# Inverse roots of GroupNorm (all groups) and of the last block's LayerNorm (in a column) with variance and running product in PSUM

## The chip, the cores and the metric

The kernel runs on one core of a Trainium2 chip. The metric is the device time of one execution in microseconds (us). Below, PE is TensorE, DVE is VectorE, ACT is ScalarE, POOL is GpSimd, and SP is SyncE, which issues the DMAs. Each engine works through its own list of instructions in order; an instruction waits until the semaphores that it needs are set, and everything behind it on that engine waits with it.

## What is computed

One block of a sequence model (2048 tokens, 1024 channels) with two token mixers, of which three things matter here:

```
h = rmsnorm(x) * (1 + scale) + shift
p = h @ w_in                                   # all inputs of both mixers
# mixer A: u = causal conv(val * sigmoid(gate)), then LayerNorm over the 1024 channels of a token
u = (u - mean(u)) * rsqrt(var(u) + LN_EPS) * ln_g + ln_b
y_conv = (silu(u) * silu(og)) @ w_conv_out
# mixer B: RWKV-7 scan per head of 64 channels, then GroupNorm over the 64 channels of a head and token
o = (o - mean(o)) * rsqrt(var(o) + GN_EPS) * gn_g + gn_b
y_rwkv = ((o + bonus) * silu(r_og)) @ w_rwkv_out
m = sigmoid(g_conv) * y_conv + sigmoid(g_rwkv) * y_rwkv
out = rmsnorm(x + gate * (m @ w_out))
```

The change concerns the two `rsqrt` of LayerNorm and GroupNorm.

## The kernel before

**Tiling and stages.** The 2048 tokens are worked in NB = 4 blocks of TB = 512, and the heads of mixer B in 4 groups of four heads, so that there are 16 groups of tokens and heads. A big fp32 product is three passes of 128x128x512 matmuls: each operand is split into a high and a low part (`h_hi`, `h_lo`, `w_hi`, `w_lo`, `w_c`; all write the tile `ps_main`), and hi x hi, lo x hi and hi x lo are summed. The `w_in` product of all blocks comes first and lasts until about 2150 us. Beside it run, block by block, the conv and its LayerNorm, and for each group a scan chain on PE, ACT and DVE (`group`, L1160: tiles `As`, `Tn`, `uv`, `xo`, `S`), then that group's GroupNorm. The three output products (`ro` for mixer B, `co` for mixer A, `o` for `w_out`) come last and are done by a fast matrix scheme (`wino`, L1910): seven products of half-size operands, in the order 0, 1, 6, 4, 2, 3, 5, whose operands are sums of tiles (`cells<-cells`, then `h_lo<-cells,h_hi`; for weights `w_c<-w_raw,w_c`) and whose results are added into `mr`, `mrh` and `cells` (`mr<-ps_main,mr`, `mr<-fc,mr`). While the last groups are still in their chains, PE is filled with the `ro` product of the first two blocks.

**What sets the order.** A planner in the same file runs while the kernel is built. Tasks are generators that `yield` conditions; `note` (L118 to L185) keeps a model of when each engine, tile and DMA will be free, and the next instruction of every engine is chosen from that. So the order of each engine is fixed before the kernel runs, and a change of one step moves others far from it. In the model, DVE and POOL exclude each other when the DVE instruction has more than one input in SBUF, or is a fast copy or `tensor_scalar` from SBUF to SBUF (`both_`).

**The steps that the change touches.** `rsteps` (L380) is the inverse root: a first guess by integer arithmetic on the bits, then three rounds of Newton's method with three DVE instructions each (y*y, times -x/2, plus 1.5 times y). `rsqrt` (L392) runs it at once with a temporary `rs_t`. In GroupNorm (end of `group`, from L1348) the four tokens-by-heads columns give a 128x16 tile of variances `gst`; L1370 calls `rsqrt(rs, st, lt, nc.vector)` with `rs` = `grs`, and POOL then multiplies `uv` by `grs`; PE transposes the result (`late<-ident,uv`), and after the gates it goes to DRAM. In the LayerNorm of the last block (`lnorm_first`, L1468), `ones @ qs` (`late<-lnq,ones`) puts the sum over channels into all 128 rows, so that the root works on a 128x512 tile in which all rows are the same (`lnr`, `lnt`, `lnq`); it is stored to `rl_d` and loaded again later by `last_u` (L2126), which normalizes the last block with it. All recorded instructions carry the line of one helper, L196, so one goes by the names of tiles. `aux` and `late` are PSUM tiles: `late` has one bank (L671), `aux` rotates over two.

Of the kernel before, what the change touches and what calls it, by code (L numbers as in the profile page):

```python
# [9 lines left out]
F32 = mybir.dt.float32  # L10
F32R = mybir.dt.float32r
I32 = mybir.dt.int32
AF = mybir.ActivationFunctionType
ALU = mybir.AluOpType
# [4 lines left out]
P = 128  # L19
D = 1024  # L20
KT = D // P
TB = 512
NTT = TB // P
# [5 lines left out]
RMS_EPS, LN_EPS, GN_EPS, L2_EPS = 1e-6, 1e-5, 64e-5, 1e-12  # L29
# [30 lines left out]
AHEAD = 0.7  # L60
# [24 lines left out]
def hybrid_block(ctx: ExitStack, tc: tile.TileContext, x, x_t, vecs, convk, w2a2, final_g, ada, w_in, w_co, w_ro, w_o, crow, out,  # L85
                 seq=2048, groups=(0, 1, 2, 3), phase2=True, dbg=None):
    NB = seq // TB
# [167 lines left out]
    def ok(*aps):  # L255
        ks = [key(a) for a in aps]
        return lambda: max(ready[q] for q in ks)
# [5 lines left out]
    def idle(name, us):  # L263
        return lambda: vt[name] - us
# [4 lines left out]
    def bank(tag, n=1):  # L269

        def f():
            for t_, past in tags.items():
                if t_.startswith(tag + "_"):
                    free_ = sorted((max(ready.get(q, 0.0), used.get(q, 0.0)) for q in past), reverse=True)
                    m = BANKS[tag] - n
                    return free_[m] if len(free_) > m else 0.0
            return 0.0

        return f

    def both(*ws):

        def f():
            r = [w() for w in ws]
            return None if None in r else max(r)

        return f

    def burst(*ws):
        w = both(*ws)  # L290

        def f():
            r = w()
            if r is None:
                return r
            return r + lag[0]

        return f
# [59 lines left out]
    u_dram = scratch("u_d")  # L358
    xT_dram = scratch("xT")
    xrow_d = [dp.tile([TB], F32, name=f"xrow{b}", tag=f"xrow{b}") for b in range(NB)]  # L360
    rl_d = dp.tile([P, TB], F32, name="rl_d", tag="rl_d")

    grow_d = dp.tile([D], F32, name="grow_d", tag="grow_d")

# [15 lines left out]
    def rsteps(y, x_, t, eng=None):  # L380
        eng = eng or nc.vector
        eng.tensor_scalar(out=y.bitcast(I32), in0=x_.bitcast(I32), scalar1=-0.5, scalar2=float(0x5F3759DF),
                          op0=ALU.mult, op1=ALU.add)
        for _ in range(3):
            yield
            eng.tensor_tensor(out=t, in0=y, in1=y, op=ALU.mult)
            yield
            eng.scalar_tensor_tensor(out=t, in0=t, scalar=-0.5, in1=x_, op0=ALU.mult, op1=ALU.mult)
            yield
            eng.scalar_tensor_tensor(out=y, in0=t, scalar=1.5, in1=y, op0=ALU.add, op1=ALU.mult)  # L390

    def rsqrt(y, x_, pool, eng, t=None):  # L392
        if t is None:
            t = pool.tile(list(x_.shape), F32, name="rs_t", tag="rs_t")
        for _ in rsteps(y, x_, t, eng):
            pass
# [763 lines left out]
    def group(G, before):  # L1160
# [201 lines left out]
        for half in range(2):  # L1362
# [2 lines left out]
            nc.scalar.activation(Dm.rearrange("p (a b) n -> p a b n", a=2), O16[:, half * 2:half * 2 + 2], AF.Square)  # L1365
            yield ok(Dm)
            nc.vector.tensor_reduce(out=st[:, half * 8:half * 8 + 8], in_=Dm, axis=AX.X, op=ALU.add)
        nc.vector.tensor_scalar(out=st, in0=st, scalar1=1.0 / 64, scalar2=GN_EPS, op0=ALU.mult, op1=ALU.add)
        yield idle("DVE", AHEAD + 0.1)
        rsqrt(rs, st, lt, nc.vector)  # L1370
        yield ok(rs)
        nc.gpsimd.tensor_tensor(out=O16, in0=O16, in1=bc(rs), op=ALU.mult)
        yield ok(uv)
# [94 lines left out]
    def lnorm_first(b, hx, ys=None):  # L1468

        def yload(j):  # L1470
            yj = hx.take("lny")
            nc.sync.dma_start(yj, y_dram[b][j])
            if b + 1 == NB:
                ready[key(yj)] += SLACK
            return yj

        eng = nc.vector if b + 1 == NB else nc.gpsimd
        if ys is None:
            yield hx.room(3, 1)
            ys, nxt = yload(0), yload(1)  # L1480
            for j in range(1, KT):
                yj = nxt
                if j + 1 < KT:
                    yield hx.room(1, 1)
                    nxt = yload(j + 1)
                yield ok(ys, yj)
                eng.tensor_tensor(out=ys, in0=ys, in1=yj, op=ALU.add)
                hx.give(yj)
        yield burst(ok(ys), free, bank("late"))
        ps = pl.tile([P, TB], F32, name="late", tag="late")  # L1490
        nc.tensor.matmul(ps, ones, ys, start=True, stop=True)
        mean = ys
        nc.scalar.copy(mean, ps)
        yield hx.room(2, 1)
        nxt, qs = yload(0), None
        for j in range(KT):
            yj = nxt
            if j + 1 < KT:
                yield hx.room(1, 1)
                nxt = yload(j + 1)  # L1500
            yield ok(yj, mean)
            eng.tensor_tensor(out=yj, in0=yj, in1=mean, op=ALU.subtract)
            yield both(ok(yj), hx.room(1))
            yq = hx.take("lnq")
            nc.scalar.activation(yq, yj, AF.Square)
            nc.sync.dma_start(y_dram[b][j], yj)
            hx.give(yj)
            if j == 0:
                qs = yq
            else:  # L1510
                yield ok(yq)
                eng.tensor_tensor(out=qs, in0=qs, in1=yq, op=ALU.add)
                hx.give(yq)
        yield burst(ok(qs), free, bank("late"))
        ps = pl.tile([P, TB], F32, name="late", tag="late")
        nc.tensor.matmul(ps, ones, qs, start=True, stop=True)
        nc.vector.tensor_scalar(out=qs, in0=ps, scalar1=LN_EPS, scalar2=None, op0=ALU.add)
        yield hx.room(2, 1)
        rl, rt = hx.take("lnr"), hx.take("lnt")
        for n, _ in enumerate(rsteps(rl, qs, rt)):  # L1520
            if n % 3 == 0:
                yield idle("DVE", AHEAD + 0.1)
        hx.give(qs, rt)
        hx1.give(mean)
        if b + 1 == NB:
            yield ok(rl)
            nc.sync.dma_start(rl_d, rl)
            hx.give(rl)
            return

        for j in range(KT):
            yield hx.room(3, 1)
            yj, ct, th = yload(j), hx.take("lnc"), hx.take("lnth")
            nc.sync.dma_start(ct, co_dram[b][j])
            yield ok(yj, rl)
            eng.tensor_tensor(out=yj, in0=yj, in1=rl, op=ALU.mult)
            yield ok(yj)
            nc.scalar.activation(th, yj, AF.Tanh, scale=hlg[:, j:j + 1], bias=hlb[:, j:j + 1])
            nc.scalar.activation(yj, yj, AF.Identity, scale=vc("conv_ln_g", j), bias=vc("conv_ln_b", j))
            yield ok(yj)  # L1540
            nc.vector.scalar_tensor_tensor(out=yj, in0=th, scalar=1.0, in1=yj, op0=ALU.add, op1=ALU.mult)
            hx.give(th)
            yield ok(yj, ct)
            eng.tensor_tensor(out=yj, in0=yj, in1=ct, op=ALU.mult)
            hx.give(ct)
            yield ok(yj)
            nc.sync.dma_start(u_dram[b][j], yj)
            hx.give(yj)
        hx.give(rl)
# [192 lines left out]
    with tc.manual_schedule():  # L1742
# [383 lines left out]
        def last_u():  # L2126
            yield when(lambda: side[1].done and turn[0] >= 2)
            yield uc.room(4)
            rl = uc.take()
            nc.sync.dma_start(rl, rl_d)  # L2130
            for j in range(KT):
                yield uc.room(3)
                yt, ct, th = [uc.take() for _ in range(3)]
# [174 lines left out]
```

## Time and profile before

| | us |
|---|---|
| three runs | 2682.25, 2669.76, 2681.33; median 2681.33 |
| the profiled execution | 2679.79 |
| its span in the trace | 2677.9 |
| PE busy in the span | 2591.1 (97%) |
| DVE busy | 2177.5 (81%) |
| POOL busy | 1330.8 (50%), with nothing after about 2250 |
| ACT busy | 1191.8 (45%) |

The share of the span is an average over stages. PE is what bounds most of the run, and what a change can win is in the places where PE stands idle. PE's granted clock is shown as a share of full speed: 1.00 is full, and it falls after a pause.

### The profile page before, as it was taken

The numbers are of one execution on the slowest core, as the hardware profiler recorded it, in microseconds if no ns is written. First come the engines' busy times: TensorE is split into PE (matmuls) and PEld (weight loads), VectorE is DVE, ScalarE is ACT, GpSimd is POOL, SyncE is SP. The second block draws the span as 40 slices with busy tenths as digits, with TensorE's granted clock in tenths as the row PEclk, the third lists the DMA queues.
The fourth block names the chain that finished last, engine by engine and source line by source line (L and its number), as shares of the span: only waits on it lengthen the run. The fifth ranks groups of instructions, "written<-read, shape, count | busy, mean of one in ns | idle before, by whom it ended". The sixth has DMA issues, their size and how long they took to land. (4 is left out here: it accounts for less than half of the span.)

```text
span 2677.9 us, 50719 instructions
## 1 busy us (share of the span) xinstructions
PE 2591.1 (97%) x18328; PEld 2082.4 (78%) x18328; DVE 2177.5 (81%) x3645; ACT 1191.8 (45%) x2315; POOL 1330.8 (50%) x1828
## 2 busy tenths in 40 slices
PE   8999999999999999999999999999999998999997
PEld 6777887777877888788888877878887776778786
DVE  6796889788879887878698878888888698898687
ACT  6444454543434434434444433434444454456443
POOL 3585848462658383827573756493727484000000
PEclk9999999999999999999999999999999998999999
DMA  9888778786787688967877878786766778798974
GB/s 365 293 311 303 252 260 300 246 282 229 245 278 243 223 287 262 323 204 267 281 251 233 283 258 262 224 316 207 266 197 213 241 261 299 248 328 309 349 270 159
DMA packets 390693, 711.59 MB, mean 266 GB/s; under 512 B 137493, under 2 KB 141929, under 8 KB 390442
## 3 DMA queue, kind: packets, MB, share of 16 engines
q1 hardware_dynamic: 390442, 708.35, 78.0%
q8 instruction: 144, 2.36, 0.3%
q14 instruction: 107, 0.88, 0.1%
HBM read 493.82 MB, written 213.26 MB: 264 GB/s over the span
## 5 line engine op out<-in xcount | busy, mean ns | idle before, releaser
L196 PE MATMUL ps_main<-h_hi,w_lo 128*128 128x512 f32 x2304 | 924.6, 401 | 5.2 <-POOL w_lo L196 3.8
L196 PE MATMUL ps_main<-h_hi,w_hi 128*128 128x512 f32 x2304 | 923.3, 401 | 4.9 <-DMA w_hi<-kh_in 4.2
L196 PE MATMUL ps_main<-h_lo,w_hi 128*128 128x512 f32 x2304 | 923.1, 401 | 0.0
L196 DVE SCALAR_TENSOR_TENSOR acc<-u,ck,acc 128x512 f32<-128x512 f32 x928 | 698.9, 753 | 26.8
L196 PEld LDWEIGHTS ps_main<-h_hi,w_hi 128*128 128x128 f32 x2304 | 434.7, 189 | 103.4 <-issue 10.7
L196 PEld LDWEIGHTS ps_main<-h_hi,w_lo 128*128 128x128 f32 x2304 | 434.9, 189 | 103.0 <-issue 5.7
L196 PEld LDWEIGHTS ps_main<-h_lo,w_hi 128*128 128x128 f32 x2304 | 434.8, 189 | 92.8 <-issue 5.3
L196 PE MATMUL ps_main<-h_hi,w_c 128*128 128x512 f32 x896 | 290.2, 402 | 7.9 <-DVE mr L196 4.7
L196 POOL TENSOR_TENSOR itmp<-La,TT 128x126 f32<-128x126 f32 (+22 forms) x496 | 205.3, 414 | 46.3 <-issue 13.2
L196 POOL TENSOR_TENSOR TT<-TT,itmp 128x126 f32<-128x126 f32 (+22 forms) x496 | 204.8, 413 | 38.8
L196 ACT ACTIVATE th<-ps_main 128x512 f32<-128x512 f32 x160 | 95.5, 597 | 281.0 <-PE ps_main L196 255.4
L196 PEld LDWEIGHTS ps_main<-h_hi,w_c 128*128 128x128 f32 x896 | 171.0, 191 | 51.1 <-issue 4.3
L196 PE MATMUL ps_main<-h_lo,w_c 128*128 128x512 f32 x448 | 180.5, 403 | 13.8 <-DVE h_lo L196 13.7
L196 POOL TENSOR_TENSOR w_lo<-w_st,w_hi 128x1024 fp32r<-128x1024 f32 x57 | 137.9, 2419 | 102.0 <-ACT w_hi L196 86.4
L196 ACT COPY uv<-xo 64x256 f32<-64x256 f32 (+1 forms) x192 | 80.9, 438 | 208.4 <-PE xo L196 153.6
L196 DVE SCALAR_TENSOR_TENSOR S<-xo,pe,Se 64x64 f32<-64x64 f32 x512 | 123.1, 280 | 49.0 <-PE xo L196 38.1
L196 PE MATMUL ps_main<-w_c,h_hi 128*128 128x512 f32 x448 | 140.0, 393 | 0.0
L196 ACT CAST w_c<-w_raw 128x512 fp32r<-128x512 f32 x168 | 102.3, 619 | 73.5 <-DMA w_raw<-wk_o 28.9
L196 DVE TENSOR_TENSOR As<-aux,maskA 128x512 f32<-128x512 f32 x128 | 82.4, 686 | 49.4 <-PE aux L196 48.8
L196 PEld LDWEIGHTS ps_main<-h_lo,w_c 128*128 128x128 f32 x448 | 85.8, 192 | 35.3 <-DVE h_lo L196 16.1
L196 ACT ACTIVATE Se<-S,pe 128x128 f32<-128x128 f32 x256 | 88.7, 395 | 40.1 <-DVE S L196 38.8
L196 ACT ACTIVATE t<-ps_main,mu 128x512 f32<-128x512 f32 x96 | 65.8, 686 | 80.3 <-PE ps_main L196 80.0
(301 smaller groups left out, 4525.4 us busy)
## 6 DMA issues: line engine op xcount, KB each, us to landing
w_hi<-kh_in SPq DMA_DIRECT2D x219, 512.0 KB
w_lo<-kl_in SPq DMA_DIRECT2D x219, 512.0 KB
w_st<-w_in_t SPq DMA_DIRECT2D x73, 512.0 KB
kh_in<-w_hi SPq DMA_DIRECT2D x70, 512.0 KB
kl_in<-w_lo SPq DMA_DIRECT2D x70, 512.0 KB
lny<-y_d SPq DMA_DIRECT2D x80, 256.0 KB
w_raw<-wk_o SPq DMA_DIRECT2D x56, 256.0 KB
ada_st<-ada_t SPq DMA_DIRECT2D x16, 512.0 KB
```

What stands on the lines that cost most here:

```text
L196: r = f(*a, **k)
```

## The change

A new `proot` does the same three rounds with ten DVE instructions, all in a row, with x and the temporary t in PSUM and only y in SBUF: each of the three-operand steps then has at most one input in SBUF. In all 16 GroupNorms the variance is written into a bank of `aux`, and the step waits for that bank. In the last block's LayerNorm the sum over channels is taken the other way round: four matmuls with the squares as weights and two columns of ones give [128 tokens, 2] each, so the variance is a 128x4 column and the root works on 4 elements a row where it had 512. A transpose, an ACT copy and a DMA put it into `rl_d` as 512 numbers, and the later load spreads them to all rows.

```diff
--- before.py
+++ after.py
@@ -358,7 +358,7 @@
     u_dram = scratch("u_d")
     xT_dram = scratch("xT")
     xrow_d = [dp.tile([TB], F32, name=f"xrow{b}", tag=f"xrow{b}") for b in range(NB)]
-    rl_d = dp.tile([P, TB], F32, name="rl_d", tag="rl_d")
+    rl_d = dp.tile([TB], F32, name="rl_d", tag="rl_d")
 
     grow_d = dp.tile([D], F32, name="grow_d", tag="grow_d")
 
@@ -388,6 +388,14 @@
             eng.scalar_tensor_tensor(out=t, in0=t, scalar=-0.5, in1=x_, op0=ALU.mult, op1=ALU.mult)
             yield
             eng.scalar_tensor_tensor(out=y, in0=t, scalar=1.5, in1=y, op0=ALU.add, op1=ALU.mult)
+
+    def proot(y, x_, t):
+        nc.vector.tensor_scalar(out=y.bitcast(I32), in0=x_.bitcast(I32), scalar1=-0.5, scalar2=float(0x5F3759DF),
+                                op0=ALU.mult, op1=ALU.add)
+        for _ in range(3):
+            nc.vector.scalar_tensor_tensor(out=t, in0=y, scalar=-0.5, in1=x_, op0=ALU.mult, op1=ALU.mult)
+            nc.vector.tensor_tensor(out=t, in0=t, in1=y, op=ALU.mult)
+            nc.vector.scalar_tensor_tensor(out=y, in0=t, scalar=1.5, in1=y, op0=ALU.add, op1=ALU.mult)
 
     def rsqrt(y, x_, pool, eng, t=None):
         if t is None:
@@ -1365,9 +1373,11 @@
             nc.scalar.activation(Dm.rearrange("p (a b) n -> p a b n", a=2), O16[:, half * 2:half * 2 + 2], AF.Square)
             yield ok(Dm)
             nc.vector.tensor_reduce(out=st[:, half * 8:half * 8 + 8], in_=Dm, axis=AX.X, op=ALU.add)
-        nc.vector.tensor_scalar(out=st, in0=st, scalar1=1.0 / 64, scalar2=GN_EPS, op0=ALU.mult, op1=ALU.add)
-        yield idle("DVE", AHEAD + 0.1)
-        rsqrt(rs, st, lt, nc.vector)
+        yield both(idle("DVE", AHEAD + 0.1), bank("aux"))
+        pg = pa.tile([P, 2, TB // 2], F32, name="aux", tag="aux")
+        gx = pg[:, 0, 0:16]
+        nc.vector.tensor_scalar(out=gx, in0=st, scalar1=1.0 / 64, scalar2=GN_EPS, op0=ALU.mult, op1=ALU.add)
+        proot(rs, gx, pg[:, 1, 0:16])
         yield ok(rs)
         nc.gpsimd.tensor_tensor(out=O16, in0=O16, in1=bc(rs), op=ALU.mult)
         yield ok(uv)
@@ -1511,6 +1521,28 @@
                 yield ok(yq)
                 eng.tensor_tensor(out=qs, in0=qs, in1=yq, op=ALU.add)
                 hx.give(yq)
+        if b + 1 == NB:
+            yield burst(ok(qs), free, bank("late"))
+            ps = pl.tile([P, TB], F32, name="late", tag="late")
+            for tt in range(NTT):
+                nc.tensor.matmul(ps[:, 2 * tt:2 * tt + 2], qs[:, tt * P:tt * P + P], ones[:, 0:2], start=(tt == 0),
+                                 stop=(tt == NTT - 1), skip_group_check=True)
+            st = e2.tile([P, 5, NTT], F32, name="ss0", tag="ss0", bufs=1)
+            vs, rs, t_ = ps[:, 128:128 + NTT], st[:, 3, :], ps[:, 256:256 + NTT]
+            nc.vector.tensor_scalar(out=vs, in0=ps[:, 0:2 * NTT:2], scalar1=LN_EPS, scalar2=None, op0=ALU.add)
+            hx.give(qs)
+            hx1.give(mean)
+            proot(rs, vs, t_)
+            yield burst(ok(st), free, bank("late"), hx.room(1, 1))
+            pt = pl.tile([P, TB], F32, name="late", tag="late")
+            nc.tensor.transpose(pt[0:NTT, 0:P], rs, ident)
+            gt = hx.take("gt")
+            nc.scalar.copy(gt[0:NTT, 0:P], pt[0:NTT, 0:P])
+            yield ok(gt)
+            nc.sync.dma_start(rl_d.rearrange("(n p) -> n p", p=P), gt[0:NTT, 0:P])
+            hx.give(gt)
+            return
+
         yield burst(ok(qs), free, bank("late"))
         ps = pl.tile([P, TB], F32, name="late", tag="late")
         nc.tensor.matmul(ps, ones, qs, start=True, stop=True)
@@ -1522,12 +1554,6 @@
                 yield idle("DVE", AHEAD + 0.1)
         hx.give(qs, rt)
         hx1.give(mean)
-        if b + 1 == NB:
-            yield ok(rl)
-            nc.sync.dma_start(rl_d, rl)
-            hx.give(rl)
-            return
-
         for j in range(KT):
             yield hx.room(3, 1)
             yj, ct, th = yload(j), hx.take("lnc"), hx.take("lnth")
@@ -2127,7 +2153,7 @@
             yield when(lambda: side[1].done and turn[0] >= 2)
             yield uc.room(4)
             rl = uc.take()
-            nc.sync.dma_start(rl, rl_d)
+            nc.sync.dma_start(rl, rl_d.unsqueeze(0).broadcast_to([P, TB]))
             for j in range(KT):
                 yield uc.room(3)
                 yt, ct, th = [uc.take() for _ in range(3)]
```

The planner puts many instructions in other places. First, DVE at the root of the last block's LayerNorm. Before, it lies among the adds of the `ro` product (`mr<-ps_main,mr`) and the steps of the last group's chain (`uv<-xo,uv`, `S<-xo,pe,Se`):

```order
L196 TENSOR_SCALAR lnq<-late 128x512
L196 TENSOR_SCALAR lnr<-lnq 128x512
L196 TENSOR_TENSOR mr_5_24020<-ps_main,mr_9_24024 128x512
L196 SCALAR_TENSOR_TENSOR S_438<-xo,pe,Se 64x64 x4
L196 TENSOR_TENSOR lnt<-lnr 128x512
L196 SCALAR_TENSOR_TENSOR lnt<-lnt,lnq 128x512
L196 SCALAR_TENSOR_TENSOR lnr<-lnt,lnr 128x512
L196 TENSOR_TENSOR mr_6_24021<-ps_main,mr_10_24025 128x512
```

and after, in the chain of the group ahead of it, eleven instructions of 128x4 in a row (the next rows go on in the same way; `ss` is the column y):

```order
L196 TENSOR_TENSOR lnq<-lnq 128x512
L196 TENSOR_TENSOR uv<-xo,uv 64x256
L196 TENSOR_SCALAR late<-late 128x4
L196 TENSOR_SCALAR ss_24058<-late 128x4
L196 SCALAR_TENSOR_TENSOR late<-ss_24058,late 128x4
L196 TENSOR_TENSOR late<-late,ss_24058 128x4
L196 SCALAR_TENSOR_TENSOR ss_24058<-late,ss_24058 128x4
```

The root moves one chain earlier in DVE's list and stands in one piece.

On PE, the matmul for this variance stands before among the steps of the last group's chain:

```order
L196 MATMUL ps_main<-h_hi,w_c 128x512
L196 MATMUL xo<-S_438,KR 128x128 x2
L196 MATMUL late<-lnq,ones 128x512
L196 MATMUL ps_main<-h_hi,w_c 128x512
L196 MATMUL ps_main<-h_lo,w_c 128x512
L196 MATMUL ps_main<-h_hi,w_c 128x512 x2
```

and after in the chain of the group ahead of it (the transpose `late<-ident,ss` 4x128 of the column stands 13 `ps_main` matmuls further on):

```order
L196 MATMUL xo<-S_436,KR 128x128 x2
L196 MATMUL ps_main<-h_lo,w_c 128x512
L196 MATMUL late<-ones,lnq 128x2 x4
L196 MATMUL ps_main<-h_hi,w_c 128x512
L196 MATMUL xo<-uv,tk 128x128 x2
L196 MATMUL ps_main<-h_hi,w_c 128x512
```

Counted in `ps_main` matmuls on PE's list, the last group's chain begins 49 of them later than before, and its transposes (`late<-ident,uv`) stand 23 later.

Third, the low parts for the last of the seven `ro` products of the first two blocks. Before, two of its four stand on DVE (`h_lo_25066`, `h_lo_25163`), behind the last group's root and adds of the earlier products:

```order
L196 SCALAR_TENSOR_TENSOR mr0_2_24017<-fc_24681,mr0_2_24017 128x512
L196 TENSOR_TENSOR w_c_25108<-w_raw_23816,w_c_25108 128x512
L196 SCALAR_TENSOR_TENSOR mr0_3_24018<-fc_24682,mr0_3_24018 128x512
L196 TENSOR_TENSOR mrh_24843<-mrh_24843,mr0_10_24025 128x512
L196 TENSOR_TENSOR mrh_24882<-mrh_24882,mr0_11_24026 128x512
L196 TENSOR_TENSOR w_c_25130<-w_raw_23816,w_c_25130 128x512
L196 TENSOR_TENSOR h_lo_25066<-cells_24422,h_hi_25065 128x512
L196 SCALAR_TENSOR_TENSOR mrh_24752<-fc_24681,mrh_24752 128x512
L196 SCALAR_TENSOR_TENSOR mrh_24789<-fc_24682,mrh_24789 128x512
L196 TENSOR_TENSOR h_lo_25163<-cells_24422,h_hi_25162 128x512
```

and two on POOL. After, all four stand on POOL (`h_lo_24987`, `h_lo_24999`, `h_lo_25016`, `h_lo_25059`), the last of them behind the multiplication by the last group's root:

```order
L196 TENSOR_TENSOR uv_22827<-uv_22827,gst_24927 128x4x256
L196 TENSOR_TENSOR w_c_24919<-w_raw_23722,w_c_24919 128x512
L196 TENSOR_TENSOR h_lo_24987<-cells_24541,h_hi_24986 128x512
L196 TENSOR_TENSOR h_lo_24999<-cells_24541,h_hi_24998 128x512
L196 TENSOR_TENSOR w_c_24953<-w_raw_23722,w_c_24953 128x512
L196 TENSOR_TENSOR w_c_24975<-w_raw_23733,w_c_24975 128x512
L196 TENSOR_TENSOR h_lo_25016<-cells_24541,h_hi_25015 128x512
L196 TENSOR_TENSOR uv_22827<-uv_22827,grs_24928 128x4x256
L196 TENSOR_TENSOR w_c_25009<-w_raw_23733,w_c_25009 128x512
L196 TENSOR_TENSOR w_c_25049<-w_raw_23722,w_c_25049 128x512
L196 TENSOR_TENSOR h_lo_25059<-cells_24541,h_hi_25058 128x512
```

What moved is the low parts from DVE to POOL, around `uv<-uv,grs`. On DVE the next such instruction after the last root is now `h_lo_25127`, for the first `co` product; it stands 22 rows behind the root.

## The prediction

> **What bounds the kernel now.** I read the busy times first, then the run in stretches, then what PE waited for, then the rows of the steps that are changed. Engines' busy time over the whole span:
>
> ```profile
> PE 2591.1 (97%) x18328; PEld 2082.4 (78%) x18328; DVE 2177.5 (81%) x3645; ACT 1191.8 (45%) x2315; POOL 1330.8 (50%) x1828
> ```
>
> PE is idle for 2677.9 - 2591.1 = 86.8 us in all, so a change on DVE can win only where PE stands still. The roots that are changed lie in all blocks, but the busy times by stretch show that the idle time near them lies late, from 2160 us on (columns: PE, weight load, DVE, ACT, POOL busy, then PE's granted clock, DMA share, GB/s):
>
> ```profile
> 2160.00:2200.00 40.00, 35.61 (x233) 28.03 (x233) 36.97 (x56) 22.75 (x49) 40.00 (x27) 1.00 0.65 213
> 2200.00:2210.00 10.00, 9.13 (x62) 6.80 (x61) 7.45 (x16) 5.69 (x13) 10.00 (x8) 1.00 0.95 319
> 2210.00:2230.00 20.00, 16.37 (x64) 11.97 (x64) 19.62 (x25) 6.62 (x13) 18.61 (x14) 0.91 0.77 259
> 2230.00:2252.00 22.00, 13.86 (x55) 10.00 (x54) 19.48 (x27) 7.16 (x13) 9.88 (x6) 0.86 0.84 272
> 2252.00:2320.00 68.00, 66.17 (x277) 53.14 (x275) 58.89 (x96) 36.15 (x63) 0.00 (x0) 0.97 0.87 302
> 2320.00:2350.00 30.00, 26.01 (x102) 20.41 (x102) 27.48 (x45) 11.17 (x19) 0.00 (x0) 0.89 0.69 213
> 2350.00:2530.00 180.00, 178.94 (x772) 144.70 (x771) 141.17 (x244) 101.77 (x191) 0.00 (x0) 1.00 0.95 343
> ```
>
> From 2160 to 2252 PE is idle for 4.39 + 0.87 + 3.63 + 8.14 = **17.03 us**, while DVE is busy for 83.52 of 92 us, POOL for 78.49. There DVE, together with POOL, is the limit. Where PE is fed it does one recorded matmul in 178.94 / 772 = 0.23 us (last row). What PE waited for between 2160 and 2360:
>
> ```profile
> PE ps_main L196 <- DVE h_lo L196: 14.8, 5, 5.6
> PE ps_main L196 <- DVE mr L196: 4.7, 5, 1.7
> ```
>
> The single waits, from PE's timeline:
>
> ```profile
> 2176.58 0.50 PE L196 MATMUL ps_main<-h_hi,w_c 128*128 128x512 f32 x1 [1.69 <-DVE mr L196]
> ...
> 2193.99 0.71 PE L196 MATMUL xo<-S,KR 128*128 128x128 f32 x4 [1.63 <-DVE S L196]
> ...
> 2226.58 0.47 PE L196 MATMUL ps_main<-h_hi,w_c 128*128 128x512 f32 x1 [1.51 <-DVE mr L196]
> ...
> 2246.40 0.79 PE L196 MATMUL ps_main<-h_lo,w_c 128*128 128x512 f32 x1 [5.63 <-DVE h_lo L196]
> ...
> 2250.55 0.80 PE L196 MATMUL ps_main<-h_lo,w_c 128*128 128x512 f32 x1 [2.50 <-DVE h_lo L196]
> ```
>
> The first three stand right behind pieces of the two roots on DVE, as the next rows show; the last two wait for low parts at the end of DVE's backlog.
>
> **The GroupNorm root: durations.** The 16 roots, by their tiles (minimum, median, maximum in ns):
>
> ```profile
> L196 DVE TENSOR_SCALAR gst<-gst x32: 174/176/1226, 297.9 to 2217.4; 128x16 f32<-128x16 f32 x32
> L196 DVE TENSOR_TENSOR rs_t<-grs x48: 174/178/2332, 313.8 to 2225.2; 128x16 f32<-128x16 f32 x48
> ```
>
> An instruction of 16 elements takes 0.176 us, or about 1.2 us when something holds it up. In the last group, on DVE and then on POOL:
>
> ```profile
> 2217.39 1.23 DVE L196 TENSOR_SCALAR gst<-gst 128x16 f32<-128x16 f32 x1
> ...
> 2219.14 0.71 DVE L196 TENSOR_SCALAR grs<-gst 128x16 int32<-128x16 int32 x1
> 2219.88 1.19 DVE L196 TENSOR_TENSOR rs_t<-grs 128x16 f32<-128x16 f32 x1
> 2221.11 1.21 DVE L196 SCALAR_TENSOR_TENSOR rs_t<-rs_t,gst 128x16 f32<-128x16 f32 x1
> 2222.35 1.20 DVE L196 SCALAR_TENSOR_TENSOR grs<-rs_t,grs 128x16 f32<-128x16 f32 x1
> 2223.59 1.20 DVE L196 TENSOR_TENSOR rs_t<-grs 128x16 f32<-128x16 f32 x1
> 2224.83 0.17 DVE L196 SCALAR_TENSOR_TENSOR rs_t<-rs_t,gst 128x16 f32<-128x16 f32 x1
> ...
> 2225.66 0.17 DVE L196 SCALAR_TENSOR_TENSOR grs<-rs_t,grs 128x16 f32<-128x16 f32 x1
> ```
>
> ```profile
> 2222.24 2.52 POOL L196 TENSOR_TENSOR h_lo<-cells,h_hi 128x512 fp32r<-128x512 f32 x2
> 2225.98 1.90 POOL L196 TENSOR_TENSOR uv<-uv,grs 128x1024 f32<-128x1024 f32 x1 [1.22 <-DVE grs L196]
> ```
>
> The slow ones end when POOL stops (2222.24 + 2.52 = 2224.76): while POOL reads SBUF they run at its pace, and at 0.17 us as soon as it is idle. These eleven sum to 1.23 + 0.71 + 1.19 + 1.21 + 1.20 + 1.20 + 5 x 0.17 = 7.59 us. Does an operand in PSUM free them? Two groups with one input in PSUM and one in SBUF, many of them beside a busy POOL, and behind them one with both inputs in SBUF:
>
> ```profile
> L196 DVE TENSOR_TENSOR mr<-ps_main,mr x28: 677/691/694, 2163.9 to 2482.7; 128x512 f32<-128x512 f32 x28
> L196 DVE SCALAR_TENSOR_TENSOR S<-xo,pe,Se x512: 250/282/294, 258.8 to 2206.7; 64x64 f32<-64x64 f32 x171
> ...
> L196 DVE SCALAR_TENSOR_TENSOR mr<-fc,mr x44: 678/684/1791, 2197.9 to 2585.5; 128x512 f32<-128x512 f32 x44
> ```
>
> The first two never took longer than 0.694 and 0.294 us, while the third, as long by its median, has a maximum of 1.791. So I take them as free of it. No row shows 16 elements in PSUM. Bounds: below, 0.161 us (a 128x4 one, next fence); above, the 0.282 us of `S<-xo,pe,Se` with 64 elements. I take 0.2, nearer to the 16-element row: 11 x 0.2 = 2.2 us, **5.4 us less** in the last group (between 4.5 and 5.8).
>
> [...]
>
> **The LayerNorm root.** On DVE before, its first two pieces and the last row:
>
> ```profile
> 2167.90 0.69 DVE L196 TENSOR_SCALAR lnq<-late 128x512 f32<-128x512 f32 x1 [0.44 <-PE late L196]
> 2168.63 0.82 DVE L196 TENSOR_SCALAR lnr<-lnq 128x512 int32<-128x512 int32 x1
> ...
> 2170.97 1.43 DVE L196 TENSOR_TENSOR lnt<-lnr 128x512 f32<-128x512 f32 x1
> 2172.43 1.67 DVE L196 SCALAR_TENSOR_TENSOR lnt<-lnt,lnq 128x512 f32<-128x512 f32 x1
> ...
> 2191.44 1.67 DVE L196 SCALAR_TENSOR_TENSOR lnr<-lnt,lnr 128x512 f32<-128x512 f32 x1
> ```
>
> ```profile
> L196 DVE SCALAR_TENSOR_TENSOR rt<-rt,vs x6: 161/162/164, 2435.8 to 2454.4; 128x4 f32<-128x4 f32 x6
> ```
>
> Two at 0.69 and 0.82, three rounds at 1.43 to 1.67 each: about 1.5 + 3 x 4.7 = 15.6 us. As a 128x4 column the eleven take 0.162 to 0.282 each, 1.8 to 3.1; at 0.2, 2.2 us: **13.4 us of DVE less**. The four small matmuls, the transpose, the ACT copy and the wider load replace one 128x512 matmul and a store of 256 KB by one of 2 KB. ACT is 45% busy, so its copy is covered; SP's two issues stay two. PE's four matmuls and a transpose cost at most five times the 0.275 us of a small one, against two recorded passes of 0.594: nothing either way. If a wait comes with them (`late` has one bank, DVE then holds it for 2.2 us instead of 0.69), it is 0 to 1.5 us.
>
> **What of this is on PE's path.** DVE loses 13.4 + 5.4 = 18.8 us of work in a stretch where PE waits for it.
> - The three waits right behind roots (1.69 + 1.63 + 1.51) go: **-4.8**. The remaining small ones in the 17.03 us, 17.03 - 4.83 - 8.13 = 4.1 us, stand elsewhere: kept.
> - The two waits for `h_lo` go, 5.63 + 2.50: **-8.1**. The changed order has these two on POOL. The last stands there behind `uv<-uv,grs` (1.90 us) and two `w_c`, which in the trace of before take:
>
> ```profile
> 2227.84 3.44 POOL L196 TENSOR_TENSOR w_c<-w_raw,w_c 128x512 fp32r<-128x512 f32 x2
> 2231.24 1.75 POOL L196 TENSOR_TENSOR h_lo<-cells,h_hi 128x512 fp32r<-128x512 f32 x1
> ```
>
>   So it ends 0.2 + 1.9 + 3.44 + 1.75 = 7.3 us behind the root. PE's matmul for it stands 21 `ps_main` matmuls, about 4.8 us at 0.23 apiece, behind transposes that wait for the same `uv`, so at 0.2 + 1.9 + 0.4 (their own time) + 4.8 = 7.3: just in time, with nothing to spare.
> - The clock: 0.97 over the 68 us after these waits is 0.03 x 68: **-2.0**. (The 0.86 before them is mostly paid while PE is idle.)
> - A new wait: the first `co` product needs `h_lo_25127`, 22 rows behind the root on DVE at 0.68 to 1.2, some 18 to 20 us; PE reaches it 60 matmuls behind the transposes, 2.5 + 60 x 0.23 = 16.3. Between 0 and 4 us, I take **+3**.
> - Waits for the banks of `aux` (16 times) and `late`: **+1** (0 to 3).
>
> What is late next is the same kind of thing that is late at 2320 to 2350 (4 us of idle, clock 0.89): DVE's low parts for `co`, which I leave as they are. In the other 15 groups PE is kept busy by the `w_in` product: nothing. The sum is -4.8 - 8.1 - 2.0 + 3 + 1 = -10.9 against the profiled execution's own 2679.79: 2668.9, **2669**. That execution lies 1.5 us below the median of the runs (2681.33), and the three runs lie 12.5 apart; about 0.5% (13.4 us) is what a measurement can tell from no change here.
>
> **The rivals.**
> - *DVE was not the limit (0.23).* DVE itself waits for loads there,
>
> ```profile
> 2247.53 0.69 DVE L196 SCALAR_TENSOR_TENSOR mrh<-fc,mrh 128x512 f32<-128x512 f32 x1 [1.19 <-DMA fc<-gr_d]
> ```
>
>   and the new wait for `co` takes their place with its clock loss: -8.1 and -2 come back, and the small ones give -4.8 + 4: about 2679. For it: the order on POOL has nothing to spare. Against: both `h_lo` were behind a backlog of `mr` and `w_c` that shrinks by 18.8 us.
> - *More is won (0.25).* All 17.03 us of idle and 2.0 of clock, and of the 4 us at 2320 to 2350 a half with its clock (0.11 x 30 = 3.3, half): 17 + 2 + 3.7 = 22.7, less 1: about 2658. For it: DVE has 18.8 us less, more than PE's idle time. Against: in the changed order half of `co`'s low parts still follow closely.
> - *The roots hold PSUM banks that PE needs (slower, 0.12).* `aux` rotates over two banks, and PE's second next `aux` tile after each root must wait for the root's last instruction. If DVE lags the planner there, PE, which has nothing else in order, waits 16 times, each at the 1.63 us of PE's wait for `S`: +26, and 2669 + 26 = 2695. It decides from about 0.7 us per root, where it takes back the whole gain. For it: nothing else in the trace of before writes `aux` from DVE. Against: the planner waits for the bank before it places a root, and PE waited only 1.6 us, once, where it waited for `S` in this stretch.
> - *The change does not do what it says (0.08)*, as PSUM operands of this size are held up like SBUF ones: the LayerNorm's 13.4 us remain, half of the gain: about 2674.
>
> **How the numbers follow.** The forecast has 0.32. The likeliest time is **2669**; the range takes in "more is won" with its upper bounds and the half of the slower case: **2654 to 2688**. Faster by over 0.5% is below 2668: "more is won" and nearly half of the forecast, **0.40**. Slower by over 0.5% is above 2694.7: **0.12**. The rest, **0.48**.
>
> **What would show it.** Right: eleven instructions on `aux` and `grs` at 0.2 us each in the last group, though POOL is busy; the column root at 2.2 us in one piece; PE idle from 2160 to 2252 (or where the same products end) below 8 us, and no wait over 2 us for `h_lo` of the `ro` product. Wrong: PE's waits move to `late`, `aux` or POOL's `h_lo`; root instructions over 0.5 us; or idle time that only moves to the first `co` product.

## The result, and the profile after

The changed kernel took 2684.22 us (median of 21 runs, 2677.94 to 2690.7), the kernel before 2675.28 us (21 runs, 2669.76 to 2682.25): a ratio of **1.0032, 95% interval 1.0023 to 1.0041**, some 8.5 us slower. Faster by 11 us had been forecast. The profiled execution of after took 2684.82 us, near its median; that of before, at 2679.79, lies 4.5 us above its own.

Busy times over the span (2683.1 us) of after:

```profile
PE 2593.5 (97%) x18335; PEld 2085.2 (78%) x18335; DVE 2132.8 (79%) x3641; ACT 1194.3 (45%) x2316; POOL 1331.4 (50%) x1832
```

DVE works 44.7 us less, as it should, and PE is idle for 2683.1 - 2593.5 = 89.6 us where it was 86.8. The roots themselves do what the change says; the GroupNorm root's groups of after, with minimum, median and maximum in ns, and then the LayerNorm column's:

```profile
L196 DVE SCALAR_TENSOR_TENSOR aux<-grs,aux x48: 178/178/180, 310.0 to 2234.4; 128x16 f32<-128x16 f32 x48
L196 DVE TENSOR_TENSOR aux<-aux,grs x48: 182/182/183, 310.3 to 2234.7; 128x16 f32<-128x16 f32 x48
L196 DVE SCALAR_TENSOR_TENSOR grs<-aux,grs x48: 174/174/176, 310.5 to 2234.9; 128x16 f32<-128x16 f32 x48
```

```profile
L196 DVE SCALAR_TENSOR_TENSOR late<-ss,late x3: 166/166/166, 2153.3 to 2154.5; 128x4 f32<-128x4 f32 x3
L196 DVE TENSOR_TENSOR late<-late,ss x3: 170/170/170, 2153.5 to 2154.7; 128x4 f32<-128x4 f32 x3
```

The maximum of 1.2 to 2.3 us that stood here before is gone: no instruction of these roots is held up by POOL any more, the longest takes 0.183 us. The time by stretch, in after (PE, weight load, DVE, ACT, POOL busy; PE's granted clock, DMA share, GB/s):

```profile
0.00:1300.00 1300.00, 1267.81 (x9386) 1018.27 (x9387) 1018.72 (x1718) 586.96 (x1132) 754.74 (x1028) 1.00 0.81 274
1300.00:2100.00 800.00, 785.55 (x5868) 634.16 (x5867) 657.00 (x1098) 318.84 (x636) 470.06 (x704) 0.99 0.75 246
...
2160.00:2256.00 96.00, 87.41 (x763) 68.15 (x763) 78.23 (x142) 47.72 (x95) 81.35 (x56) 0.98 0.76 260
2256.00:2288.00 32.00, 26.35 (x99) 20.03 (x100) 29.34 (x47) 19.14 (x34) 0.81 (x1) 0.89 1.00 372
...
2323.00:2355.00 32.00, 25.56 (x92) 19.84 (x93) 28.74 (x48) 10.83 (x19) 0.00 (x0) 0.84 0.68 220
```

From 2160 to 2256, where the same products run that took until 2252 before, PE is idle for 8.6 us instead of 17.0. But from 2256 to 2288 it is idle for 5.65 us, and from 2323 to 2355 for 6.4 us with the clock at 0.84. In the stretches of before that match these two it was idle for nothing, and for 4.8 us with the clock at 0.89:

```profile
2252.00:2285.70 33.70, 33.70 (x139) 27.23 (x138) 29.58 (x49) 20.72 (x36) 0.00 (x0) 0.94 0.99 352
2320.00:2351.00 31.00, 26.18 (x103) 20.57 (x104) 28.48 (x47) 11.33 (x20) 0.00 (x0) 0.89 0.70 219
```

So most of what is won up to 2256 is lost again behind it. The first 2100 us were thought to cost nothing. From 1300 to 2100 PE is idle for 14.45 us in after, against

```profile
1300.00:2100.00 800.00, 787.89 (x6268) 634.14 (x6268) 662.89 (x1105) 319.75 (x638) 468.33 (x710) 1.00 0.75 248
```

12.11 us before. By itself this difference says little: in experiment 12 below, which keeps the order of before and is faster than both kernels, PE is idle for 17.43 us there. What PE waited for between 2160 and 2360 in after, and the single waits on its timeline, one of them in block three:

```profile
PE ps_main L196 <- DVE h_lo L196: 10.8, 5, 5.4
PE ps_main L196 <- POOL w_c L196: 4.6, 4, 2.2
PE ps_main L196 <- ACT h_hi L196: 4.0, 2, 3.3
```

```profile
1500.69 0.50 PE L196 MATMUL ps_main<-h_hi,w_hi 128*128 128x512 f32 x1 [2.50 <-DVE vv L196]
...
2258.02 0.50 PE L196 MATMUL ps_main<-h_lo,w_c 128*128 128x512 f32 x1 [2.46 <-DVE h_lo L196]
...
2345.11 0.80 PE L196 MATMUL ps_main<-h_hi,w_c 128*128 128x512 f32 x1 [3.29 <-ACT h_hi L196]
```

The waits behind the roots are gone and waits for POOL's `w_c` (4.6 us) stand where they stood. The wait at 2258 is the one forecast for the first `co` product; that at 2345 is new. The one at 1500 lies in the stretch that was thought to cost nothing. On DVE and POOL in after, ahead of it:

```profile
1495.23 0.17 DVE L196 SCALAR_TENSOR_TENSOR grs<-aux,grs 128x16 f32<-128x16 f32 x1
1495.32 1.47 DVE L196 SCALAR_TENSOR_TENSOR KR<-k,v,E 128x256 f32<-128x256 f32 x2
1496.89 0.78 DVE L196 SCALAR_TENSOR_TENSOR rk<-r,hrk,ta 128x512 f32<-128x512 f32 x1
1497.59 2.39 DVE L196 SCALAR_TENSOR_TENSOR lny<-lnth,lny 128x512 f32<-128x512 f32 x1
1499.90 0.74 DVE L196 SCALAR_TENSOR_TENSOR vv<-ps_main,v,t 128x511 f32<-128x511 f32 x1
```

```profile
1497.08 2.35 POOL L196 TENSOR_TENSOR uv<-uv,grs 128x1024 f32<-128x1024 f32 x1
```

The root is done at 1495.4 and POOL's long multiplication by it starts at 1497.08. In the new order `lny`, with both inputs in SBUF, stands beside that one: it takes 2.39 us, where it took 0.69 us at 1501.67 in before, and ends only after POOL's instruction has (1497.08 + 2.35 = 1499.43). `vv`, which frees the bank that PE needs, is behind it. Such single places can differ from run to run, so experiments had to say how much of the 8.5 us is order and how much is anything else.

### The profile page after: what moved, and what is told of

It reads as the page before. It is cut to its first block, busy times and chain, and to the rows that moved or that the text cites. A ratio compares the mean times of both kernels' runs of the same rounds, so it can differ in the third digit from the quotient of the medians.

```text
span 2683.1 us, 50782 instructions
## 1 busy us (share of the span) xinstructions
PE 2593.5 (97%) x18335; PEld 2085.2 (78%) x18335; DVE 2132.8 (79%) x3641; ACT 1194.3 (45%) x2316; POOL 1331.4 (50%) x1832
## 4 chain that ended last, share of the span: by engine, by line
PE 80%; DMA 5%; DVE 5%; POOL 4%; issue 3%; ACT 1%; SPq 1%; DVEq 0%; POOLq 0%; ACTq 0%
PE ps_main L196 65%; PE aux L196 7%; PE xo L196 5%; PE late L196 3%; SPq L196 1%; DMA w_lo<-kl_in 1%; DVE As L196 1%; POOL w_lo L196 1%; DVE acc L196 1%; PE ps_f L196 0%; DMA w_b<-w_ro_t 0%; DMA dn<-dN 0%; DMA As<-dT 0%; POOL h_lo L196 0%; DMA lny<-y_d 0%
## 5 line engine op out<-in xcount | busy, mean ns | idle before, releaser
L196 POOL TENSOR_TENSOR w_lo<-w_st,w_hi 128x1024 fp32r<-128x1024 f32 x60 | 145.4, 2423 | 105.6 <-ACT w_hi L196 80.6
L196 PE MATMUL ps_main<-h_lo,w_c 128*128 128x512 f32 x448 | 180.9, 404 | 10.9 <-DVE h_lo L196 10.8
```

The costliest lines, as they stand in the source:

```text
L196: r = f(*a, **k)
```

## Experiments

Each was timed in five rounds against the kernel before on the same chip; they are numbered as their runs are, and no run has the number 3. "Measured" is the ratio to the kernel before, with its 95% interval. The theory: **order**, that is, the roots win what they can, and the planner's new order of everything else loses more. Rivals: **off the path**, the roots were never what PE waited for; **banks**, roots that hold PSUM banks make PE wait; **LayerNorm**, the loss comes from the column.

**Experiment 1: GroupNorm in PSUM, order of before.** The planner's model gets the old instructions and their costs, and the new ones are issued past it; the variance's scaling moves down to the root.

```diff
-        nc.vector.tensor_scalar(out=st, in0=st, ...)
+        note("DVE", "tensor_scalar", st, [st], 0.0, [st])
         yield idle("DVE", AHEAD + 0.1)
-        rsqrt(rs, st, lt, nc.vector)
+        pnote(rs, st, tp, False)              # the ten old instructions, for the model alone
+        pg = pa.tile([P, 2, TB // 2], F32, name="aux", tag="aux")
+        gx = pg[:, 0, 0:16]
+        tc.nc.vector.tensor_scalar(out=gx, in0=st, ...)
+        proot_raw(rs, gx, pg[:, 1, 0:16])
```

> All 16 GroupNorm roots in PSUM, but the planner is told the old costs, so that every engine keeps the order of before; LayerNorm as before. Theory 'order' (the faster roots win what they can, the planner's new order loses more): 2 to 6 us faster than before, ratio 0.998 to 0.999. Theory 'off the path' (the roots were never what PE waited for): within 1 us, ratio 1.000. Theory 'banks' (roots hold PSUM banks that PE needs): slower, ratio 1.002 or more.

Measured: 1.0006 (0.9991 to 1.002). All lists but DVE's are those of before, word for word. No loss by banks shows, so that rival falls, and no gain shows either: in its own order the old root's stalls cost next to nothing. For the last group its trace shows why, on PE's timeline:

```profile
2215.41 1.01 PE L196 MATMUL ps_main<-h_hi,w_c 128*128 128x512 f32 x2 [2.07 <-POOL w_c L196]
...
2229.04 0.47 PE L196 MATMUL ps_main<-h_hi,w_c 128*128 128x512 f32 x1 [0.32 <-DVE mr L196]
...
2239.31 0.80 PE L196 MATMUL ps_main<-h_lo,w_c 128*128 128x512 f32 x1 [5.50 <-DVE h_lo L196]
...
2243.54 0.79 PE L196 MATMUL ps_main<-h_lo,w_c 128*128 128x512 f32 x1 [2.58 <-DVE h_lo L196]
```

The wait for `mr` behind the root falls from 1.51 to 0.32 us, and the two for `h_lo` stay. The one for POOL's `w_c` grows to 2.07; in before it was

```profile
2221.09 0.72 PE L196 MATMUL ps_main<-h_hi,w_c 128*128 128x512 f32 x2 [1.03 <-POOL w_c L196]
```

**Experiment 2: both changes, order of before.** The same, and the LayerNorm column with four small matmuls in place of one; the column is stored straight from SBUF.

```diff
+            note("PE", "matmul", ps, [ones, qs], 0.0, [ones])
+            for tt in range(NTT):
+                tc.nc.tensor.matmul(ps[:, 2 * tt:2 * tt + 2], qs[:, tt * P:tt * P + P], ones[:, 0:2], ...)
...
+            proot_raw(col, vs, t_)
...
+            tc.nc.sync.dma_start(rl_d.rearrange("(n p) -> p n", p=P), col)
```

> Both changes (GroupNorm roots in PSUM, the last block's LayerNorm root as a column) in the order of before; the column goes to DRAM straight from SBUF, without the transpose. DVE has some 18 us less to do between 2160 and 2230. Theory 'order': the waits of the prediction go, 5 to 13 us faster, ratio 0.995 to 0.998. Theory 'off the path': within 2 us of before. Theory 'banks': slower than before, as the experiment with GroupNorm alone.

Measured: 1.0021 (1.0007 to 1.0036), slower. Its trace gives the reason, on PE's and on DVE's timeline:

```profile
2201.83 0.79 PE L197 MATMUL xo<-uv,tk 128*128 128x128 f32 x2 [5.67 <-DVE uv L197]
```

```profile
2199.90 0.69 DVE L197 SCALAR_TENSOR_TENSOR mr<-fc,mr 128x512 f32<-128x512 f32 x1 [6.25 <-DMA fc<-gr_d]
```

DVE waits 6.25 us for a load of `fc`, and PE for DVE. On SP's queue that load stands right behind the store of 512 pieces of 4 bytes:

```profile
2187.76 0.43 SPq L1574 DMA_DIRECT2D rl_d<-ss  x1
2188.24 1.04 SPq L197 DMA_DIRECT2D fc<-gr_d  x2
```

Issued at 2188.2 to 2189.3, it was there at 2199.9. So this was my store and not the change; experiment 9 undoes it.

**Experiment 4: the GroupNorm change in the last block alone**, LayerNorm as changed, planner free.

```diff
+        if b + 1 == NB:
...
+            proot(rs, gx, pg[:, 1, 0:16])
+        else:
...
+            rsqrt(rs, st, lt, nc.vector)
```

> The change with GroupNorm's root in PSUM only in the last block (4 of 16 groups), LayerNorm as changed, the planner free. The order of the first three blocks is that of before. Theory 'order': the loss before 2100 us (about 6 us between the two profiles, compared at equal work of PE) is gone, so 5 us or more faster than the changed kernel: ratio to before 0.996 to 1.001. Theory 'banks': three quarters of the loss go too, ratio about 1.001. If the loss lies in the last stage instead: ratio about 1.003, as the changed kernel.

Measured: 1.0005 (0.9988 to 1.0022). Against 1.0032 for the full change the loss is gone; the intervals all but part (1.0022 and 1.0023). That speaks for the order of the first three blocks as the place of most of it; the last block's order differs from that of after as well, so it does not settle it.

**Experiment 5: the old GroupNorm roots in the order of after.** The reverse of the first.

```diff
+        note("DVE", "tensor_scalar", gx, [st], 0.0, [st])
+        pnote(rs, gx, pg[:, 1, 0:16], True)   # the ten new instructions, for the model alone
+        tc.nc.vector.tensor_scalar(out=st, in0=st, ...)
+        root_raw(rs, st, lt.tile([P, 16], F32, name="rs_t", tag="rs_t"))
```

> The changed kernel with the GroupNorm roots back in SBUF (old instructions), in exactly the order of the changed kernel, LayerNorm as changed. Theory 'order': slower than the changed kernel by what the roots win, 2 to 6 us, ratio to before 1.004 to 1.006. Theory 'off the path': as the changed kernel, ratio 1.003. Theory 'banks': faster than the changed kernel, ratio 1.000 to 1.002.

Measured: 1.0069 (1.0049 to 1.0089), from five runs. The new order with old GroupNorm roots, and the LayerNorm as changed, costs 0.69%, some 18 us; against the 1.0032 of after, the new roots are worth 0.37% in that order, some 10 us. In experiment 1 they were worth nothing that shows. A likely reason, which no run tests: the planner's model has the stalls, so the order of before left room for them, and that of after doesn't.

**Experiments 6 and 7: each part alone, planner free.** (The diffs are the parts of the change.)

> Only the GroupNorm part of the change, planner free. Theory 'order': the whole order changes with it, and most of the changed kernel's loss is here: ratio 1.002 to 1.005. Theory 'LayerNorm' (the column root, its transpose and its earlier place are what costs): ratio 0.999 to 1.001.

> Only the LayerNorm part, planner free; the order differs from before near this root only. Theory 'order': about as before, ratio 0.998 to 1.001, since the first three blocks keep their order. Theory 'LayerNorm': ratio 1.002 to 1.004.

Measured: GroupNorm alone 1.0037 (1.0021 to 1.0052), LayerNorm alone 0.9991 (0.9976 to 1.0007). The loss comes with the GroupNorm part, which changes the order from the first block on; the LayerNorm theory falls. The trace of the first has the same wait for `vv` in block three as after (2.49 us; in experiment 5 it is 4.23):

```profile
1500.85 0.80 PE L196 MATMUL ps_main<-h_hi,w_hi 128*128 128x512 f32 x1 [2.49 <-DVE vv L196]
```

```profile
1505.64 0.50 PE L196 MATMUL ps_main<-h_hi,w_hi 128*128 128x512 f32 x1 [4.23 <-DVE vv L196]
```

No trace in the order of before has it. So it belongs to that order and not to one execution.

**Where in the run the loss lies.** PE's busy time, weighted with its granted clock, sums to nearly the same in every trace (2572 to 2576 us), so one can ask when a given part of this work is done. The first 2040 us of it are done at 2098.3 us in after, at 2098.4 in experiment 5 and at 2098.3 in experiment 6, which have the same order up to there. In the eight traces with the order of before up to there (before and experiments 1, 2, 7, 9, 10, 11 and 12) they are done between 2082.7 and 2093.6 us. So the new order loses some 5 to 16 us ahead of the last groups. One trace stands against it: experiment 4, in the order of before up to 1900 us, comes to 2099.3; its profiled execution is the slowest of its twelve (2689.39 us, median 2678.01). From that point to the end before takes 586.5 us and after 584.8: of the 10.9 us forecast there, these two traces show 1.7.

**Experiments 8 and 13: other orders without any new instruction.** Only the condition for placing a GroupNorm root differs, by 0.2 us one way and 0.1 the other.

```diff
-        yield idle("DVE", AHEAD + 0.1)
+        yield idle("DVE", AHEAD + 0.3)        # experiment 13: AHEAD
```

> The kernel before, with all its old instructions; only the condition under which the planner places a GroupNorm root is eased by 0.2 us (idle ahead 0.3 instead of 0.1), which changes the order about as much as the change does (1913 rows of PE's list differ, 1790 there). If any new order costs what the changed one costs: ratio 1.002 or more, or otherwise off 1 by as much on the other side. If the loss belongs to what the change's order does: ratio within 0.999 to 1.001.

> The kernel before with all its old instructions, the condition for placing a GroupNorm root tightened (idle ahead 0.0 instead of 0.1); 1199 rows of PE's list differ. If the order of before is one picked out of many, so that nearly every other order loses: ratio 1.002 to 1.010, as the first change of this kind (1.0109) and as the changed kernel. If orders scatter on both sides: as likely below 1.000.

Measured: **1.0109** (1.0088 to 1.0129) and **1.0061** (1.0046 to 1.0076). Two orders taken for no reason of their own lose 29 and 16 us (six runs each). So a new plan can cost this much without any new instruction, and the order of before is better than both. It need not cost it: experiments 4 and 7 were planned anew near the end and show no loss. Nor does the loss lie in one place: in experiment 8 the first 2040 us of PE's work are done at 2100.0 us, in experiment 13 at 2090.6, as in the order of before, and there the loss comes later.

**Experiment 9: both changes in the order of before, with a cheap store.** 128 pieces of 16 bytes; the tokens then stand in another order in `rl_d`, so the last block is normalized with other tokens' roots.

```diff
-            tc.nc.sync.dma_start(rl_d.rearrange("(n p) -> p n", p=P), col)
+            tc.nc.sync.dma_start(rl_d.rearrange("(p n) -> p n", n=NTT), col)
```

> Both changes in the order of before, as in the second experiment, but the column goes to DRAM in 128 pieces of 16 bytes instead of 512 of 4, which leaves the tokens in another order in rl_d (the last block's normalization uses the wrong token's root). Theory 'the store was the cost' (the loads of fc behind it landed 11 us after issue): the wait of 5.7 us for uv at 2202 is gone and the ratio is 0.998 to 1.000; the waits of 5.5 and 2.5 us for h_lo stay, since they end with loads. Theory 'the column itself costs': ratio 1.002 again.

Measured: **0.9972** (0.9956 to 0.9987). The change of instructions, with the order held, makes the kernel faster by about 7.5 us.

**Experiment 12: the same with the tokens in order.** DVE transposes the column, and four DMAs store 4 rows of 128 bytes each.

```diff
+            tc.nc.vector.memset(rt[:, 0:32], 0.0)
+            tc.nc.vector.tensor_copy(rt[:, 0:NTT], col)
+            tc.nc.vector.transpose(rl[:, 0:32], rt[:, 0:32])
...
+            for i in range(4):
+                tc.nc.sync.dma_start(rl_d.rearrange("(n i c) -> i n c", i=4, c=32)[i], rl[32 * i:32 * i + NTT, 0:32])
```

> As the last one without the moved low parts. The gain of both changes in the old order, 0.997, holds if the four small stores do not hold up the loads behind them; with them as costly as the 512 pieces of 4 bytes it is 1.002.

Measured: **0.9974** (0.9961 to 0.9986), median 2669.63. This version beats both kernels. (Its column goes to DRAM another way than in after; with the way of after, experiment 7 shows no loss.) It also shows what the saved DVE time bought. On PE:

```profile
2214.66 1.09 PE L197 MATMUL ps_main<-h_hi,w_c 128*128 128x512 f32 x2 [2.06 <-POOL w_c L197]
...
2239.00 0.79 PE L197 MATMUL ps_main<-h_lo,w_c 128*128 128x512 f32 x1 [5.97 <-DVE h_lo L197]
...
2243.11 0.79 PE L197 MATMUL ps_main<-h_lo,w_c 128*128 128x512 f32 x1 [2.46 <-DVE h_lo L197]
```

and on DVE and POOL, behind the last root:

```profile
2213.57 0.17 DVE L410 SCALAR_TENSOR_TENSOR grs<-aux,grs 128x16 f32<-128x16 f32 x1
2213.66 0.68 DVE L197 TENSOR_TENSOR mr<-ps_main,mr 128x512 f32<-128x512 f32 x1
2218.85 0.69 DVE L197 TENSOR_TENSOR mr<-ps_main,mr 128x512 f32<-128x512 f32 x1 [4.51 <-PE ps_main L197]
2219.46 2.98 DVE L197 TENSOR_TENSOR mr<-mr,mr 128x512 f32<-128x512 f32 x2
...
2238.26 0.69 DVE L197 TENSOR_TENSOR h_lo<-cells,h_hi 128x512 fp32r<-128x512 f32 x1
```

```profile
2213.34 2.50 POOL L197 TENSOR_TENSOR w_c<-w_raw,w_c 128x512 fp32r<-128x512 f32 x2
2215.80 2.53 POOL L197 TENSOR_TENSOR h_lo<-cells,h_hi 128x512 fp32r<-128x512 f32 x2
2218.28 1.91 POOL L197 TENSOR_TENSOR uv<-uv,grs 128x1024 f32<-128x1024 f32 x1
```

The two waits for `h_lo` are as long as before, 5.97 and 2.46 us against 5.63 and 2.50, though the two roots take DVE some 18 us less ahead of them. DVE now stands idle for 4.51 us waiting for a product of PE, PE waits for POOL's `w_c`, and POOL takes up `grs` only 4.5 us after it is there, since it first has its own `w_c` and `h_lo` to do. The adds that keep DVE busy until `h_lo` start with that product, at 2218.85, and run for 19 us to 2238. PE and DVE are in step again at that product, so PE's wait for `h_lo` stays, however soon the root was done.

**Experiments 10 and 11: those two low parts moved**, in the kernel before and in that of experiment 12: the first to POOL, ahead of its waits for loads, the second up by three places on DVE.

```diff
             hl_ = ch.take()
             nc.scalar.copy(hl_[0], src)
+            if early:                         # the two instructions, past the planner
+                (tc.nc.gpsimd if first else tc.nc.vector).tensor_tensor(out=hl_[1], in0=src, in1=hl_[0]..., op=ALU.subtract)
```

> The kernel before, old roots and old order, with two instructions moved: of the two low parts that PE waits for at 2246 and 2250 the first goes to POOL, ahead of its waits for loads, and the second stands three places earlier on DVE, ahead of two adds that wait for loads of fc. Theory 'DVE's list' (the waits come from what stands in front of these two on DVE, whatever the roots take): the wait of 5.6 us for h_lo goes, one of about 5 us stays for the second, which ends about 4 us earlier than now; 3 to 5 us faster, ratio 0.998 to 0.999. Theory 'loads' (PE would wait for weights or other loads there anyway): the waits reappear on w_c, ratio 1.000.

> Both changes in the order of before, with the same two low parts moved; the column is transposed by DVE and stored in 4 DMAs of 4 rows, so that rl_d holds the tokens in order. If both gains add (7 us by the roots in the old order, 4 by the move): ratio 0.995 to 0.997. If the move only shifts the wait: 0.997, as with the cheap store alone.

Measured: 0.9991 (0.9978 to 1.0004) and 0.9988 (0.9974 to 1.0001): neither parts from 1, and the second shows no gain over experiment 12. The wait of 5.97 us is gone, and others have come, as PE's timeline of experiment 11 shows:

```profile
2230.20 0.47 PE L197 MATMUL ps_main<-h_hi,w_c 128*128 128x512 f32 x1 [2.12 <-DVE mr L197]
...
2238.66 0.50 PE L197 MATMUL ps_main<-h_hi,w_c 128*128 128x512 f32 x1 [1.80 <-ACT h_hi L197]
...
2242.52 0.80 PE L197 MATMUL ps_main<-h_lo,w_c 128*128 128x512 f32 x1 [3.36 <-DVE h_lo L1882]
```

That is 7.3 us in place of 8.4. Part of it comes from an add on DVE with both inputs in SBUF, beside POOL:

```profile
2218.70 5.09 DVE L197 TENSOR_TENSOR mr<-mr,mr 128x512 f32<-128x512 f32 x1
```

```profile
2219.47 2.53 POOL L197 TENSOR_TENSOR w_c<-w_raw,w_c 128x512 fp32r<-128x512 f32 x2
2221.96 1.27 POOL L197 TENSOR_TENSOR h_lo<-cells,h_hi 128x512 fp32r<-128x512 f32 x1
2223.78 1.74 POOL L1882 TENSOR_TENSOR h_lo<-cells,h_hi 128x512 fp32r<-128x512 f32 x1 [0.55 <-ACT h_hi L197]
```

With the add behind it, it takes 5.69 us, against 2.98 in experiment 12. But the moved `h_lo` (L1882) starts only as this add ends, and what POOL does before it stands there in experiment 12 too; in experiment 10, with the same move, the two adds take 3.17 us. So the delay is not shown to come from the move, and experiment 11 does not settle what the move alone is worth.

## Why the prediction was wrong, step by step

Two steps failed: a term that was set to nothing, the order of the other 15 groups, and the reading of DVE's busy time near the end as a backlog that any saving shortens.

- **Durations: right.** 0.174 to 0.182 us for a GroupNorm instruction and 0.161 to 0.170 for the column, where 0.2 was taken, with POOL busy or not. Ten instructions of the root at 0.18 make 1.8 us in the last group, no longer held up. That an operand in PSUM keeps such an instruction free had been read from the rows of `mr` and `S`, and the trace agrees: the eleven of the last group stand at 2232.75 to 2235.05 in after, beside a POOL that is busy from 2231.13 to 2236.16. One input in SBUF did not by itself keep an instruction free: in before `gst<-gst`, with one input in SBUF and its output there too, took 1.23 us beside a busy POOL in the last group, against a median of 0.176. In the new root, where no instruction has all its operands in SBUF, none took over 0.183 us. That an operand in PSUM makes such an instruction slower does not show: 0.178 us for `aux<-grs,aux` in after against 0.176 for `rs_t<-rs_t,gst` in before.
- **Waits right behind the roots, -4.8: right with the order held.** In experiment 12 the three are no longer there or down to 0.3 us, one of 2.06 us for POOL's `w_c` stands near by, and the kernel is 7 us faster in all. In the changed order waits for `w_c` of 4.6 us took their place, for which the sum had no term.
- **The two waits for `h_lo`, -8.1: right for the changed kernel, wrong in one of its two reasons.** They go in after, since the low parts stand on POOL, as I had read from the order. The other reason was wrong: I read "DVE is busy for 83.5 of 92 us" and "PE waits for DVE" as one backlog that any saving ahead of it shortens. It is not one: the adds before `h_lo` wait for a product of PE, which waits for POOL. With the order held the waits stay to within 0.4 us (experiments 1 and 12). That was the first rival (DVE is not the limit), although I gave loads as its reason and the rows show PE and POOL.
- **The clock, -2.0: wrong.** It is at 0.89 from 2256 to 2288 and at 0.84 from 2323 to 2355, lower than in the matching stretches of before (0.94 and 0.89).
- **The new wait at the first `co` product, +3: right in place, short in size**, 2.46 + 0.83 + 1.36 = 4.65 us against 0 to 4 forecast; and the next one, 3.29 us at 2345 with the clock at 0.50 from 2345 to 2347 behind it, was not seen.
- **"In the other 15 groups ... nothing": wrong, and the largest.** The roots there indeed win nothing that shows (experiment 1), but their change made the planner order 2100 us anew. The first 2040 us of PE's work then end 7 us later than in the trace of before. The new order with the old roots costs 0.69% in all (experiment 5), and two orders made for no reason cost 1.09% and 0.61%. In the prediction the order was read at three places near the end; what it does to the rest of the run was set to zero.
- **The slower rival, PSUM banks: wrong.** Experiment 1 holds the same banks and shows no loss. The forecast's +1 for waits for banks is too small for these intervals to show.

That 2684 lies within the stated 2654 to 2688 is luck: its slow end was put there for half of the banks' case, not for an order that costs.

What stays open: why both parts together in the old order win 0.26% to 0.28% where GroupNorm alone shows nothing (1.0006) and LayerNorm alone, planned anew, 0.09% (the intervals just allow a sum); and which of the new waits in the first three blocks make up the loss, since one profile of each kernel can't part them from those that come and go from run to run.

## What to carry to other kernels

Where a planner sets the order, a change of instructions is two changes, and they can be measured apart: give the planner the old costs and issue the new instructions, and the other way round. Here the instructions won 0.27% and the new order lost more than that. Busy time ahead of a wait is a backlog only back to that engine's last idle time: look for that idle time, and for who ended it, before work ahead of it is counted as a saving. And an instruction that is held up only while another engine does work that is needed next anyway can cost next to nothing: here the root's stalls ended with POOL's own list, which had to be done before the result was used, and the kernel without them took as long (experiment 1: 1.0006, 0.9991 to 1.002).

## What was not expected of the hardware

A store of 512 pieces of 4 bytes from one column, 2 KB in all, held the load behind it on the same queue until DVE had waited 6.25 us for it; stored as 128 pieces of 16 bytes, or four times 4 rows of 128 bytes, the ratio was 0.9972 and 0.9974 against 1.0021, and with the 16 bytes (experiment 9) the chain that ended last has no load in it from 2195.9 to 2229.4 us. And a short wait can cost more than itself. Behind the wait of 2.50 us for `vv` in after, PE's clock (the third number from the end) was granted at half for 3.4 us:

```profile
1490.00:1498.00 8.00, 8.00 (x36) 6.38 (x34) 7.52 (x19) 3.60 (x7) 7.76 (x10) 1.00 0.43 153
1501.90:1505.30 3.40, 3.40 (x22) 3.08 (x23) 1.44 (x3) 0.38 (x1) 3.09 (x7) 0.50 0.82 291
1505.40:1510.00 4.60, 4.60 (x34) 3.64 (x34) 3.58 (x6) 1.08 (x2) 3.79 (x8) 1.00 0.47 146
```

The sixteen small matmuls `aux<-KR,BK` that begin at 1501.81 take 2.02 us, and 1.16 us at 1507 with the full clock. By the clock, 3.4 us at half add an estimated 1.7 us to the 2.5. Not every wait brings this: behind the one of 2.20 us for `w_c` at 2209 the clock stayed at 1.00 (2209 to 2220 us). So PE's clock falls after some pauses here, not after each.
